# Sharing a PSUM bank between the key and value second layers of a compression pair, and storing the last prompt tile's rows from SyncE's queue

## The chip, the cores and the metric

The kernel runs on one NeuronCore of a Trainium2 chip. The metric is the device time of one execution in microseconds (us); lower is better. The kernel before takes 892.15 us (median of three runs, 891.99 to 892.65). Every row below comes from one profiled execution of it.

Engines are named as the profile names them: PE is TensorE (PEld its weight loads), DVE is VectorE, ACT is ScalarE, POOL is GpSimd, SP is SyncE. A name with q at its end, such as ACTq, is the instruction queue of that engine, where DMA issues stand.

## What is computed

One inference step of a hybrid decoder layer for 512 prompt tokens and 8 sample sequences of 8 tokens with a past of 4096 rows each. One input projection feeds an attention with three gated branches (compressed, selected, window) and a state-space branch; both are projected, gated, added and normalised. The part that the change touches is the compression of the cached keys and values: 16 rows at a time are taken with the 16 rows behind them, sent through a first layer, a SiLU and a second layer.

```python
def compress(rows, w1, b1, w2, b2, pos):
    B, N = rows.shape[:2]
    nch = N // CMP_STRIDE
    ch = rows[:, :nch * CMP_STRIDE].reshape(B, nch, CMP_STRIDE, N_KV, HEAD_DIM).astype(jnp.float32)
    h_first = jnp.einsum('bcpgd,pdh->bcgh', ch, w1[:CMP_STRIDE])
    h_second = jnp.einsum('bcpgd,pdh->bcgh', ch, w1[CMP_STRIDE:])
    h = h_first[:, :-1] + h_second[:, 1:] + (jnp.einsum('pd,pdh->h', pos, w1) + b1)
    out = jnp.einsum('bcgh,hd->bcgd', jax.nn.silu(h), w2) + b2
    ends = jnp.arange(nch - 1, dtype=jnp.int32) * CMP_STRIDE + (CMP_BLOCK - 1)
    return out, ends
```

It is called for the keys and for the values of all 8 samples (255 compressed rows each, 2 heads of 64). The attention of the samples reads `out`, two samples at a time. The prompt's attention output, multiplied by SiLU(z), goes into the output projection at the end.

## The kernel before, in words

**Stages.** The input projection and the state-space scan come first. Then the 512 prompt tokens are attended in four tiles of 128 (`prompt_tile`, i = 0 to 3), tiles 2 and 3 after the compression has been set up. The eight samples follow in `sample`: `compress` makes the compressed keys and values, `attend(w, store)` attends the pair w of samples 2w and 2w+1. The output stage ends the kernel.

**Compression.** `compress` is a generator of small steps. It goes over half samples j = 0 to 15 (sample b = j // 2, half h = j % 2); within a half, first the keys (kv = 0) and then the values (kv = 1), four steps k = 0 to 3 each. I write K0, V0 for the keys and values of sample 0, K1, V1 for sample 1, and so on. A step of `first_layer` splits its rows into a high and a low part (`evh` on ACT, `evl` on DVE; two buffers each) and runs 12 matmuls of about 256 columns on them, into a PSUM bank with the tag "mm" (two banks: one for K, one for V of a sample). Beside the steps, `compress_rows`/`compress_blocks` transpose the rows of the next half (`xt`, DVE, L892) and issue the gathers of later ones (`gc`, POOL, L1091). After the last step of a sample's keys or values, `silu2` reads the bank (ACT, tile `hs`), takes tanh (`hth`) and multiplies (DVE); `hs` has two buffers, so each is held until its second layer's matmuls have read it.

**The second layer.** `second_layer` takes one tile of the tag "ca", which has one bank. For the keys it runs two matmuls (L1165, four instructions in the profile) and ACT copies the result into `kc` (L1168, shown at L108, the line of the helper `act`); for the values it runs two matmuls (L1173, four instructions) for each half t of the rows and DVE copies each half into `vc` (L1175). `late` holds one pending second layer: K of a sample runs in step k = 1 of its own values, V of a sample in step k = 1 of the next sample's keys. `kc` and `vc` live in the pool "attend" (`self.pb`), which lies on the SBUF that the prompt's pools leave.

**Order.** A planner orders each engine's queue when the kernel is built: it takes the instructions that are ready in a simulated run of its own, those that come first in the program ahead of the others, so that steps of `compress` run between the instructions of prompt tiles 2 and 3. On the chip every queue keeps that order: what waits holds up all that stands behind it on its engine.

**The end of a prompt tile.** For the two attention branches the tile transposes the probabilities P (`p_tr`, L135), copies them to SBUF (`pt`, ACT) and multiplies them with the values (`p_acc`, L1036), once for each of i + 1 blocks of keys; the compressed branch comes last (`pcT`, L1078). DVE multiplies the sum with SiLU(z) into `ast` (L1084) and ACT's queue stores it to DRAM (`aD`, L1085). `aD` is read back by the output stage (L1610).

**After it.** `attend_setup` makes the gates (L1220) and loads `selt` (L1217, SP). `past_gather` gathers the cached rows of the selected branch (tile `g`, POOL, also L1091). `attend(w)` starts with the scores against `kc` of both samples of the pair (L1237). SP also carries the loads `y<-yD` (L1548), which the state-space output reads, and other loads of the output stage.

Of the kernel before, what the change touches and what calls it, by code (L numbers as in the profile page):

```python
# [12 lines left out]
AF = mybir.ActivationFunctionType  # L13
OP = mybir.AluOpType
# [71 lines left out]
def rr(ap, pat, **kw):  # L86
    return ap.rearrange(pat, **kw)


class Hybrid:  # L90
# [899 lines left out]
    def prompt_tile(self, i, KT, kczs, vcp, bt):  # L990

        nc, pp = self.nc, self.pp
        V = nc.vector
# [3 lines left out]
        q0 = i * 128  # L997
# [4 lines left out]
        for br in range(2):  # L1002
            P4s = []
            for g in range(2):
# [3 lines left out]
                for r in range(4):  # L1008
                    p = self.psum("S", [128, 512])
# [14 lines left out]
            for kt in range(i + 1):  # L1024
# [10 lines left out]
                for g in range(2):  # L1035
                    mm = nc.tensor.matmul(acc[gr[g]], self.kvn[:, kt, c0 + g * 64:c0 + (g + 1) * 64], PTs[g][:], start=br == 0 and kt == 0,  # L1036
                                          stop=False, skip_group_check=True)
# [9 lines left out]
        p = self.psum("S", [128, 4, 2, 64])  # L1047
# [4 lines left out]
        pv = rr(p[:], "p r g n -> p (r g) n")  # L1052
# [29 lines left out]
        st = pp.tile([128, 4, 128], F, name="ast", tag="ast", bufs=1)  # L1082
        nc.sync.dma_start(st[:], rr(self.zD[0:4], "r p t -> p r t")[:, :, q0:q0 + 128])
        V.tensor_tensor(st[:], rr(acc[:], "p (r q) -> p r q", r=4), st[:], op=OP.mult)  # L1084
        nc.scalar.dma_start(self.aD[:, :, q0:q0 + 128], st[:])  # L1085


    def gather(self, out, cache, idx):
# [67 lines left out]
                             h == 0 and wj == 0, h == 1 and wj == 15, skip_group_check=True)  # L1156
            yield

    def second_layer(self, kv, sl, out):

        nc, V = self.nc, self.nc.vector
        p2 = self.psum("ca", [128, 2, 128])
        if kv == 0:
            for g in range(2):
                nc.tensor.matmul(rr(p2[g * 64:(g + 1) * 64], "p t d -> p (t d)")[:, 0:255], self.w2[:, 0, :], sl[:, g, :],  # L1165
                                 start=True, stop=True)
            V.memset(out[:, 255:256], 0.0)
            self.act(out[:, 0:255], rr(p2[:], "p t d -> p (t d)")[:, 0:255], AF.Identity, bias=self.kb2[:], scale=0.5)  # L1168
        else:
            for t in range(2):  # L1170
                m = 128 - t
                for g in range(2):
                    nc.tensor.matmul(p2[:m, t, g * 64:(g + 1) * 64], sl[:, g, t * 128:t * 128 + m], self.w2[:, 1, :],  # L1173
                                     start=True, stop=True)
                V.scalar_tensor_tensor(out[:m, t], p2[:m, t], 0.5, self.vb2[:m, :], op0=OP.mult, op1=OP.add)  # L1175

    def compress(self, store):


        late = None  # L1180
        for j in range(2 * NB):
            b, h = divmod(j, 2)
            w = b // 2
            rows = self.compress_half(j + 1, NB) if 0 < j < 2 * NB - 1 else iter(())
            if not h:
                accs = [self.psum("mm", [128, 2, 256]) for _ in range(2)]
            xs = self.xs.pop(0)
            for kv in range(2):
                for k, _ in enumerate(self.first_layer(kv, h, xs[kv], accs[kv])):
                    for _ in range(3 if kv + k == 0 else 2):  # L1190
                        next(rows, None)
                    if k == 1 and late:
                        self.second_layer(*late)
                        late = None
                    if k == 3 and h:
                        if w not in store:
                            store[w] = [self.pb.tile([128, 2] + [256] * (1 - v) + [2, 128] * v, F, name=nm, tag=nm, bufs=1)
                                        for v, nm in enumerate(("kc", "vc"))]
                        sl = self.silu2(kv, accs[kv][:, :, 0:255], 255, self.pw, 2)
                        late = kv, sl, store[w][1][:, :, b % 2] if kv else store[w][0][:, b % 2]  # L1200
                    yield
            for _ in rows:
                pass
        self.second_layer(*late)

    def attend_setup(self):
        nc, A, cp, pb = self.nc, self.A, self.cp, self.pb
# [523 lines left out]
```

## Time and profile before

| what | value |
|---|---|
| median of three runs | 892.15 us (891.99 to 892.65) |
| the profiled execution | 889.58 us, of which the span of the core is 887.8 us |
| PE, PEld busy | 849.6 us (96%), 747.8 us (84%) |
| DVE, ACT, POOL busy | 568.8 us (64%), 426.2 us (48%), 196.0 us (22%) |
| mean granted TensorE clock over the span | 0.981 |
| the chain that ended last | PE 65%, DVE 11%, DMA 7%, issue 5%, POOL 4%, ACT 4%, SP's queue 3% |

The profiled execution lies 2.57 us below the median. The 1.78 us between its time and the span lie around the span. A wait row reads: the engine and line that waited, what it waited for, us in total, times, the longest. A timeline row reads: start in us, length in us, engine, line, instruction, output <- inputs, shapes, count, and in brackets the idle time of the engine before it and what ended that. The granted clock is in shares of full speed: 1.00 is 2.4 GHz, 0.50 is 1.2 GHz.

### The profile page before, as it was taken

The page shows a single profiled execution, that of the slowest core. Times are in us where ns is not written, and L with a number is a line of the kernel's source. Part 1 is how long each engine was busy: PE and PEld are TensorE (multiplying, and loading weights), DVE is VectorE, ACT ScalarE, POOL GpSimd, SP SyncE. Part 2 cuts the span into 40 slices and gives each one's busy share as a digit, 9 for nine tenths or more (in the row PEclk, how much of TensorE's full clock was granted, in tenths as well). Part 3 has the DMA queues.
Part 4 walks back from the last instruction along what each step waited for, and adds up shares of the span by engine and source line. Part 5 has one row for each costly group of instructions (what it writes and reads, how often), then busy time and mean ns, then how long its engine had stood idle before and what let it go on. Part 6 is the DMA issues. An engine that isn't in the chain of part 4 may idle for free.

```text
span 887.8 us, 18479 instructions
## 1 busy us (share of the span) xinstructions
PE 849.6 (96%) x7276; PEld 747.8 (84%) x7276; DVE 568.8 (64%) x1559; ACT 426.2 (48%) x876; POOL 196.0 (22%) x249
## 2 busy tenths in 40 slices
PE   8999999999999988999989999999999979999996
PEld 8999999999999967787757878787878758889885
DVE  3469973855354479988627767766764463448784
ACT  4224462223254365768535656555555565545420
POOL 0322719300042211121211323241321101200000
PEclk9999999999999979999979999999999989999999
DMA  8385526365687352323457746383726164849331
GB/s 279 95 201 165 148 67 193 113 203 150 208 247 239 135 133 96 120 96 120 148 182 216 264 164 261 120 313 116 285 97 238 61 236 145 283 129 277 109 107 48
DMA packets 116039, 151.03 MB, mean 170 GB/s; under 512 B 29352, under 2 KB 93224, under 8 KB 111600
## 3 DMA queue, kind: packets, MB, share of 16 engines
q1 hardware_dynamic: 89072, 65.02, 25.6%
q0 software_dynamic: 17824, 80.16, 25.2%
q10 hardware_dynamic: 9056, 4.67, 1.8%
q8 instruction: 57, 0.93, 0.4%
q14 instruction: 30, 0.25, 0.1%
HBM read 134.02 MB, written 19.93 MB: 173 GB/s over the span
## 4 chain that ended last, share of the span: by engine, by line
PE 65%; DVE 11%; DMA 7%; issue 5%; POOL 4%; ACT 4%; SPq 3%; POOLq 0%; DVEq 0%; ACTq 0%
PE p_mm L130 11%; PE p_mm L129 10%; PE p_mm L131 10%; PE p_tr L135 7%; PE p_S L1237 4%; PE p_ca L129 3%; PE p_ca L131 3%; PE p_ca L130 3%; DVE xt L892 2%; PE p_acc L1246 2%; DMA gc<-in_cache_kv_cmp,idx 2%; PE p_acc L1036 2%; DMA relx<-in_rel_bias 1%; DMA wraw<-in_w_in 1%; DVE evl L121 1%
## 5 line engine op out<-in xcount | busy, mean ns | idle before, releaser
L130 PE MATMUL p_mm<-evl,w1h 128*128 128x256 f32 (+1 forms) x512 | 153.8, 300 | 6.3 <-DVE evl L121 6.2
L129 PE MATMUL p_mm<-evh,w1h 128*128 128x256 f32 (+1 forms) x512 | 151.1, 295 | 1.1 <-ACT w1h L108 0.6
L131 PE MATMUL p_mm<-evh,w1l 128*128 128x256 f32 (+1 forms) x512 | 148.2, 290 | 0.9 <-DVE w1l L121 0.9
L121 DVE TENSOR_TENSOR evl<-xt,evh 128x512 fp32r<-128x512 f32 x128 | 87.0, 684 | 52.1 <-ACT evh L108 51.7
L130 PEld LDWEIGHTS p_mm<-evl,w1h 128*128 128x128 f32 x512 | 98.7, 193 | 24.8 <-DVE evl L121 13.1
L108 ACT ACTIVATE evh<-xt 128x512 fp32r<-128x512 f32 x128 | 80.1, 628 | 79.7 <-PE p_mm L131 75.2
L1091 POOL DMA_INDIRECT gc<-in_cache_kv_cmp,idx x64 | 65.5, 1024 | 206.7 <-DVE xt L892 188.9
L129 PEld LDWEIGHTS p_mm<-evh,w1h 128*128 128x128 f32 x512 | 98.9, 193 | 8.7 <-ACT kt L108 2.4
L131 PEld LDWEIGHTS p_mm<-evh,w1l 128*128 128x128 f32 x512 | 98.6, 193 | 5.8 <-issue 4.1
L892 DVE STREAM_TRANSPOSE xt<-gc 128x256 f32<-128x256 f32 x256 | 90.5, 410 | 5.2 <-DMA gc<-in_cache_kv_cmp,idx 4.6
L131 PE MATMUL p_mm<-xTh,wlo 128*128 128x288 f32 x272 | 81.0, 298 | 0.0
L130 PE MATMUL p_mm<-xTl,whi 128*128 128x288 f32 x272 | 81.0, 298 | 0.0
L129 PE MATMUL p_mm<-xTh,whi 128*128 128x288 f32 x272 | 80.9, 298 | 0.0
L108 ACT ACTIVATE pt<-p_tr 128x512 f32<-128x512 f32 x76 | 43.5, 591 | 29.3 <-PE p_tr L135 29.2
L341 DVE TENSOR_TENSOR wlo<-wraw,whi 128x512 fp32r<-128x512 f32 (+1 forms) x56 | 37.5, 728 | 25.4 <-ACT whi L108 25.4
L1091 POOL DMA_INDIRECT g<-in_cache_kv_slc,idx x32 | 32.6, 1018 | 92.9 <-PE p_acc L1246 65.7
L108 ACT ACTIVATE kt<-p_tr 128x512 f32<-128x512 f32 x72 | 40.7, 594 | 24.2 <-PE p_tr L135 24.2
L130 PEld LDWEIGHTS p_mm<-xTl,whi 128*128 128x128 f32 x272 | 51.3, 189 | 0.2 <-issue 0.2
L129 PEld LDWEIGHTS p_mm<-xTh,whi 128*128 128x128 f32 x272 | 51.3, 189 | 0.2 <-issue 0.2
L108 ACT ACTIVATE whi<-wraw 128x2048 fp32r<-128x2048 f32 (+2 forms) x24 | 37.1, 1563 | 29.9 <-DMA wraw<-in_w_in 9.4
L131 PEld LDWEIGHTS p_mm<-xTh,wlo 128*128 128x128 f32 x272 | 51.4, 189 | 0.0
L135 PE MATMUL p_tr<-cst,P 128*128 128x128 f32 x304 | 47.1, 284 | 0.6 <-ACT P L108 0.5
(527 smaller groups left out, 2105.4 us busy)
## 6 DMA issues: line engine op xcount, KB each, us to landing
wraw<-in_w_in SPq DMA_DIRECT2D x11, 1024.0 KB
wraw<-in_w_in SPq DMA_DIRECT2D x10, 512.0 KB
gD<-zst POOLq DMA_DIRECT2D x16, 288.0 KB, 3.2
tg<-gD SPq DMA_DIRECT2D x16, 288.0 KB
wn<-in_state_win_kv POOLq DMA_DIRECT2D x4, 1024.0 KB, 6.2
wor<-in_w_o SPq DMA_DIRECT2D x8, 512.0 KB
out<-in_state_win_kv SPq DMA_DIRECT2D x8, 504.0 KB
wraw<-in_w_in SPq DMA_DIRECT2D x3, 1056.0 KB
```

Of the source, the lines that this page charges most:

```text
L108: return self.nc.scalar.activation(out, in_, func, **kw)
L121: eng.tensor_tensor(lo, src, hi.bitcast(F), op=OP.subtract)
L129: mm(out, lhi, rhi, start=start, stop=False, **kw)
L130: mm(out, lhi, rlo, start=False, stop=False, **kw)
L131: mm(out, llo, rhi, start=False, stop=stop, **kw)
L135: return self.nc.tensor.transpose(out, in_, self.ident[:k, :k])
L341: (eng or self.nc.vector).tensor_tensor(lo[:, kl, :n], w[:, kl, :n], hi[:, kl, :n].bitcast(F), op=OP.subtract)
L892: self.nc.vector.transpose(out=out, in_=in_)
L1036: mm = nc.tensor.matmul(acc[gr[g]], self.kvn[:, kt, c0 + g * 64:c0 + (g + 1) * 64], PTs[g][:], start=br == 0 and kt == 0, stop=False, skip ...
L1091: self.nc.gpsimd.indirect_dma_start(out=rr(out, "c s v g d -> c (s v g d)"), out_offset=None, in_=src, in_offset=bass.IndirectOffsetOnAxis ...
L1237: mm = self.nc.tensor.matmul(out[r], self.qb[:, w, r], keys[b], start=True, stop=True)
L1246: self.nc.tensor.matmul(acc[r], PT[:, r], vals(b)[:, g * 64:(g + 1) * 64], start=start, stop=stop, skip_group_check=True)
```

## The change

Two things change. In `prompt_tile` the store of `ast` goes to SP's queue for the last tile (i = 3) and stays in ACT's queue for the others. In the compression `second_layer` becomes `second_layers`, which takes a list: it allocates one bank of "ca", gives columns 0 to 254 to the keys and columns 256 to 511 to the values, runs all matmuls of the list and then all copies. `late` becomes a list. For the first sample of a pair (b even) the keys' second layer is no longer run during the sample's own values; it waits and runs together with the values' second layer in step k = 1 of the next sample's keys. For the second sample of a pair (b odd) keys and values still run apart, at the places where they ran. The values' matmuls now all come before both copies, with the head in the outer loop and the half t in the inner one. Their number and shapes are the same.

```diff
@@ prompt_tile
         V.tensor_tensor(st[:], rr(acc[:], "p (r q) -> p r q", r=4), st[:], op=OP.mult)
-        nc.scalar.dma_start(self.aD[:, :, q0:q0 + 128], st[:])
+        (nc.sync if i == 3 else nc.scalar).dma_start(self.aD[:, :, q0:q0 + 128], st[:])
@@ second_layer
-    def second_layer(self, kv, sl, out):
+    def second_layers(self, layers):
 
         nc, V = self.nc, self.nc.vector
-        p2 = self.psum("ca", [128, 2, 128])
-        if kv == 0:
+        p2 = self.psum("ca", [128, 512])
+        pk, pv = p2[:, 0:255], rr(p2[:, 256:512], "p (t d) -> p t d", t=2)
+        for kv, sl, _ in layers:
             for g in range(2):
-                nc.tensor.matmul(rr(p2[g * 64:(g + 1) * 64], "p t d -> p (t d)")[:, 0:255], self.w2[:, 0, :], sl[:, g, :],
-                                 start=True, stop=True)
-            V.memset(out[:, 255:256], 0.0)
-            self.act(out[:, 0:255], rr(p2[:], "p t d -> p (t d)")[:, 0:255], AF.Identity, bias=self.kb2[:], scale=0.5)
-        else:
+                if not kv:
+                    nc.tensor.matmul(pk[g * 64:(g + 1) * 64], self.w2[:, 0, :], sl[:, g, :], start=True, stop=True)
+                    continue
+                for t in range(2):
+                    m = 128 - t
+                    nc.tensor.matmul(pv[:m, t, g * 64:(g + 1) * 64], sl[:, g, t * 128:t * 128 + m], self.w2[:, 1, :],
+                                     start=True, stop=True)
+        for kv, _, out in layers:
+            if not kv:
+                V.memset(out[:, 255:256], 0.0)
+                self.act(out[:, 0:255], pk, AF.Identity, bias=self.kb2[:], scale=0.5)
+                continue
             for t in range(2):
                 m = 128 - t
-                for g in range(2):
-                    nc.tensor.matmul(p2[:m, t, g * 64:(g + 1) * 64], sl[:, g, t * 128:t * 128 + m], self.w2[:, 1, :],
-                                     start=True, stop=True)
-                V.scalar_tensor_tensor(out[:m, t], p2[:m, t], 0.5, self.vb2[:m, :], op0=OP.mult, op1=OP.add)
+                V.scalar_tensor_tensor(out[:m, t], pv[:m, t], 0.5, self.vb2[:m, :], op0=OP.mult, op1=OP.add)
@@ compress
-        late = None
+        late = []
...
-                    if k == 1 and late:
-                        self.second_layer(*late)
-                        late = None
+
+                    if k == 1 and late and (b % 2 or not kv):
+                        self.second_layers(late)
+                        late = []
...
-                        late = kv, sl, store[w][1][:, :, b % 2] if kv else store[w][0][:, b % 2]
+                        late.append((kv, sl, store[w][1][:, :, b % 2] if kv else store[w][0][:, b % 2]))
...
-        self.second_layer(*late)
+        self.second_layers(late)
```

## Rows read from the trace of the kernel before

**Rows 1.** The page's engine totals: busy us, share of the span, instructions.
```profile
PE 849.6 (96%) x7276; PEld 747.8 (84%) x7276; DVE 568.8 (64%) x1559; ACT 426.2 (48%) x876; POOL 196.0 (22%) x249
```

**Rows 2.** Stretches: us; PE, PEld, DVE, ACT, POOL busy (instructions); clock, DMA, GB/s.
```profile
400.00:442.35 42.35, 40.19 (x283) 32.66 (x281) 33.27 (x92) 29.25 (x63) 9.01 (x9) 1.00 0.45 140
442.35:453.20 10.85, 9.48 (x53) 4.05 (x51) 3.93 (x13) 4.83 (x10) 0.00 (x0) 1.00 0.05 10
453.20:466.39 13.19, 10.98 (x45) 8.56 (x45) 3.68 (x15) 3.05 (x6) 3.58 (x4) 0.61 0.90 306
466.39:476.39 10.00, 10.00 (x90) 8.68 (x90) 8.85 (x34) 5.99 (x13) 4.29 (x4) 1.00 0.68 184
```

**Rows 3.** Waits from 442.35 to 466.39 us, all engines.
```profile
POOL g L1091 <- PE p_acc L1078: 19.2, 1, 19.2
DVE ast L1084 <- PE p_acc L1078: 6.8, 1, 6.8
ACT hs L108 <- PE p_ca L1173: 4.5, 1, 4.5
PE p_ca L1173 <- ACT kc L108: 1.9, 1, 1.9
```

**Rows 4.** Timeline of 366 to 474 us, the rows of the second layers.
```profile
373.77 0.65 PE L1165 MATMUL p_ca<-hs,w 128*64 128x255 f32 x4
...
442.35 0.28 PE L131 MATMUL p_mm<-evh,w1l 128*128 128x256 f32 x1
...
453.22 0.69 DVE L1084 TENSOR_TENSOR ast<-p_acc,ast 128x512 f32<-128x512 f32 x1 [6.84 <-PE p_acc L1078]
...
453.94 0.52 ACTq L1085 DMA_DIRECT2D aD<-ast  x1
...
454.50 0.47 ACT L108 ACTIVATE kc<-p_ca,kb 128x255 f32<-128x255 f32 x1 [2.46 <-DVE ml L1401]
...
455.03 0.66 PE L1173 MATMUL p_ca<-w,hs 128*128 128x64 f32 x4 [1.86 <-ACT kc L108]
...
455.73 0.29 DVE L1175 SCALAR_TENSOR_TENSOR vc<-p_ca,vb 128x128 f32<-128x128 f32 x1 [1.56 <-PE p_ca L1173]
...
458.49 1.12 PE L1173 MATMUL p_ca<-w,hs 128*127 128x64 f32 x4
459.64 0.29 DVE L1175 SCALAR_TENSOR_TENSOR vc<-p_ca,vb 127x128 f32<-127x128 f32 x1 [1.23 <-PE p_ca L1173]
459.64 0.69 ACT L108 ACTIVATE hs<-p_mm,hb 128x510 f32<-128x510 f32 x1 [4.50 <-PE p_ca L1173]
...
459.99 1.12 PE L1165 MATMUL p_ca<-hs,w 128*64 128x255 f32 x4 [0.38 <-DVE vc L1175]
...
469.98 0.60 PE L135 MATMUL p_tr<-cst,g 128*128 128x128 f32 x4
```

**Rows 5.** One matmul of the first layer on the chain that ended last: start, us.
```profile
439.95 0.12 PE p_mm L129
```

**Rows 6.** PE's waits over the whole span: the one for gathered rows.
```profile
PE p_tr L135 <- DMA g<-in_cache_kv_slc,idx: 1.2, 1, 1.2
```

**Rows 7.** POOL's queue, timeline: a gather for compression that starts after 442 us.
```profile
470.93 1.47 POOL L1091 DMA_INDIRECT gc<-in_cache_kv_cmp,idx  x1 [12.79 <-DVE xt L892]
```

**Rows 8.** SP's queue, timeline, and ACT's first reader of `y`.
```profile
437.12 0.51 SPq L1217 DMA_DIRECT2D selt<-cst  x1
...
450.86 2.69 SPq L1548 DMA_DIRECT2D y<-yD  x6
...
716.65 4.33 ACT L108 ACTIVATE ah<-y 128x576 fp32r<-128x576 f32 x4
```

**Rows 9.** Uses of `aD`: engine, operation, ns, first and last start.
```profile
L1610 SPq DMA_DIRECT2D a<-aD x4: 430/431/506, 736.6 to 738.1; - x4
```

**Rows 10.** Whose waits ended the idle time ahead of L1175: us, times.
```profile
  PE p_ca L1173: 10.3, 8
```

## The prediction

> **What bounds the kernel now.** I read the page's totals first. PE is busy for 849.6 us of 887.8, DVE for 568.8, ACT for 426.2 [rows 1]: an edit pays here only where it gives PE time back. The totals also count a matmul that runs at half clock as busy, so I went next to the table of stretches around the only place where the second layers stand in anybody's way, the end of prompt tile 3. From 400 to 442 us PE runs 283 matmuls in 42.35 us at clock 1.00, 0.150 us each, the idle time included. From 442.35 to 466.39 it runs 53 + 45 = 98 in 24.04 us; it is idle for 1.37 and then for 2.21 us, and in the second part the granted clock is 0.61, part at 1.2 and part at 2.4 GHz. From 466.39 on it runs 90 in 10 us, without idle time, at 1.00 [rows 2]. What PE did before the clock fell is in the first of the two stretches: no more than the chain of the tile's last blocks, with gaps.
>
> The waits of that stretch and the timeline say why there was nothing else to run. K0's second layer ran at 373.77, but its bank is copied out only at 454.50, behind the tile's end: DVE's L1084 at 453.22, then the store in ACT's queue at 453.94 for 0.52 us [rows 4]. For 80 us K0 holds the only bank of "ca". V0's second layer starts at 455.03, when the bank is free, and its other half at 458.49. Until both have read V0's `hs`, the silu of V1 has no buffer: ACT waits 4.5 us for L1173 [rows 3] and reads V1's bank at 459.64 [rows 4]. Until that read V2 has no bank "mm". So at 442.35 the first layer stops, with the 48 matmuls of K2's first half done, and V2's 48 start after 460. One chain, ca, hs, mm, and PE runs dry at the end of it.
>
> **The change part by part.** *One bank for K0 and V0.* It removes the allocation on which V0 waited. Both second layers run right after sample 1's first steps, long before 442 us; V0's `hs` is free when V1 wants it, V1's silu runs when its first layer is done, and V2's bank comes free some 30 us earlier. No instruction disappears, and the four of V0's first half and four of its second move out of the jam. What PE gets is other work for the gaps: V2's first half (48 matmuls), and, as K1 and V1 no longer block the banks "mm", K2's and V2's second halves (96 more), 144 x 0.12 us [rows 5] = 17.3 us. K2's silu is the next that needs a buffer from K1, and K1's second layer still waits for the bank until the tile's end. What is lost today is bounded by two ways of counting. Idle time and clock: 1.37 + 2.21 + 10.98 x (1 - 0.61) = 7.9 us. Rate: 98 x 0.150 = 14.7 us instead of 24.04, 9.3 us [rows 2]. I take the middle, 8.6 us: the rate has the usual waits in it already, but the mix is not quite the same.
>
> What is late next is the tile's end itself. K0 and V0 are copied only when `kc` and `vc` may be written, and I take that to stay at L1084's end. Then follow K0's and V0's copies, K1's matmuls in the same bank, K1's copy, and only then the scores of `attend(0)`. Priced from rows 4: copies 0.47 by ACT and 2 x 0.29 by DVE, K1's matmuls 0.65 (at full clock, the row of K0), K1's copy 0.47. No row of before has ACT and DVE reading one bank of "ca"; side by side the two copies take 0.58, one after the other 1.05. I take the dearer end, and the chain is 1.05 + 0.65 + 0.47 = 2.2 us; all of it is charged, though first-layer work may cover it. The page "PSUM — Partial Sum Buffer" of the Trainium skill, section "PSUM bank collisions raise a hardware error", says that ScalarE and VectorE must not read one bank and quadrant at the same time, so copies out of a shared bank have to be ordered one after the other; this speaks against sharing, no run here shows it yet, and by it the sum is the one with 1.05, by the other view it would be 0.5 us better.
>
> The tile's end also comes later, as first-layer matmuls stand between its blocks, and with it the gathers of `g`, for which POOL waits 19.2 us [rows 3]. The single wait of PE for such rows is 1.2 us [rows 6]; I charge half of it, 0.6, with ends 0 and, in the rival below, far more.
>
> *The store in SP's queue.* ACT gives up 0.52 us in front of K0's copy [rows 4], part of the stretch counted above, so not counted again. On SP the store waits for L1084. `selt` is issued at 437.12, ahead of it; the loads `y` may have to stand behind it, the first six of them issued at 450.86, and their reader is at 716.65 [rows 8]. `aD` is read at 736.6 [rows 9]. Both covers are over 200 us, so the move costs nothing there. If the planner puts the store ahead of `selt`, the gates (L1220) start some 2 us late; I hold it unlikely, since `selt` is ready 16 us earlier.
>
> *The other pairs.* K2, K4 and K6 move half a sample later, beside V2, V4 and V6; the pairs' scores need the odd sample's keys, which come later still. The values' matmuls no longer wait for the first of two copies; DVE has waited 10.3 us in 8 places for L1173 [rows 10], under other work of PE. Counted at nothing, between -1 (each DVE wait that stands ahead of an `evl`) and +1 us (three times half a copy chain).
>
> The sum: 8.6 - 2.2 - 0.6 = 5.8 us, against 889.58 us of the profiled execution: 883.8. The median lies 2.57 us above it, so 892.15 - 5.8 = 886.35, and I say 886.3.
>
> **The rivals.** *The planner leaves the work where it is.* The queues are ordered in its own simulated run, not by what is free on the chip. If V2 still stands behind L1084, the gaps stay and the change does less than it says: what is left is the 0.56 us from 453.94 to 454.50 and V0's matmuls, 0.66 + 1.12 us, out of the chain [rows 4], some 2.3 us: 889.9. For it: DVE and ACT are in order, and L1084 waits for 6.8 us at the head of DVE's queue [rows 3]. Against it: K0's second layer and K2's first half stand well ahead of the tile's end today.
>
> *Given back.* The time is won in the tail and lost after it: the steps that filled the tail are missing under `attend(0)`, whose chain of small operations needs them. 892, give or take 1.
>
> *Slower: too much filler, and the rows come late.* Place: the stretch between L1084 and the first transposes of `g`, 453.2 to 469.98, 16.8 us of gathering [rows 4]. PE's work for it is 21 of today's 45 matmuls, 3.2 us at 0.150, and what is left of the 144. With x of them used in the tail the rest is (144 - x) x 0.12. If the gathers `gc` for sample 3 stand behind those of `g` in POOL's queue, as today (470.93, [rows 7]), nothing else is to be had, and PE idles for 16.8 - 3.2 - (144 - x) x 0.12; at half clock 4.3 us more, as now. From x = 65 on this eats the gain (4.1 + 4.3 us). With 96 it is 7.8 + 4.3 = 12.1 us, against 9.3 won: slower by 2.8 at most, and I take 2.3: 894.5. Against it: the transposes that release `gc` belong to V2's steps, which come early now, and POOL sits idle for 19.2 us in just that time.
>
> **How the numbers follow.** The forecast has 0.58 (its own range 883 to 889.5), the planner's rival 0.13, given back 0.15, slower 0.14. Faster by over 0.2% (under 890.4 us; about what a measurement of this kernel can tell from no change) is the forecast but for 0.02, and most of the planner's rival, 0.08: 0.65 with a little of the third. The same holds what is left of these, 0.20. Slower is the last but for its mild half and some of the third: 0.15. The range goes from 882.8 (all of 9.3 us won) to 893.0 (given back, and the mild half of slower); outside lie 0.04 below and 0.12 above, with some play.
>
> **What would show it.** Right: L1165 and L1173 of sample 0 stand together before 430 us; the wait of `hs` for L1173 is gone; between the last four L1036 groups of tile 3 there are first-layer matmuls; the granted clock stays near 1.00 between 440 and 470 us; L1084 itself comes later than 453.2 us. The copy of K0 follows L1084 with no store between. Wrong: a new idle stretch of PE, with the clock at 1.2 GHz, that waits for `g` or `gc`; or the stretch unchanged with L1173 early. If PE is full there and the end of the kernel has still not moved, it is the third case.

## The result, and the profile after

The kernel after takes 904.59 us (median of four runs, 896.95 to 906.14) against 892.4 us of the kernel before beside it (four runs): ratio 1.0119, 95% interval 1.009 to 1.0149. (The ratios here and below are those on record with the runs, not quotients of medians; the two medians by themselves stand at 1.0137.) It is slower by 1.2%, where 886.3 us was forecast. Its profiled execution took 905.68 us, with a span of 903.9, 16.1 more than before. Chips differ: on two of them the kernel before itself took 907 us; every ratio below is against the kernel before on the same chip.

Engine totals of the page (busy us, share, instructions), then the four stretches of [rows 2] in the kernel after (us; PE, PEld, DVE, ACT, POOL busy; clock, DMA share, GB/s):

```profile
PE 853.7 (94%) x7276; PEld 752.0 (83%) x7276; DVE 570.5 (63%) x1559; ACT 426.5 (47%) x876; POOL 193.6 (21%) x249
```

```profile
400.00:442.35 42.35, 41.69 (x284) 32.32 (x283) 33.26 (x97) 31.26 (x68) 3.86 (x4) 1.00 0.19 63
442.35:453.20 10.85, 10.85 (x78) 7.91 (x77) 8.54 (x24) 5.64 (x12) 4.36 (x4) 1.00 0.60 193
453.20:466.39 13.19, 12.61 (x91) 10.08 (x90) 7.66 (x20) 5.28 (x10) 4.03 (x5) 1.00 0.22 56
466.39:476.39 10.00, 5.41 (x37) 4.63 (x37) 5.28 (x14) 3.58 (x8) 4.50 (x5) 0.83 1.03 354
```

I call the stretch at the end of tile 3 the jam, and first-layer work that runs in it filler. The jam that the forecast set out to fill is full: 78 + 91 = 169 matmuls where [rows 2] has 98, at clock 1.00. But a new hole stands behind it, in the stretch that was full before: PE is idle for 4.59 of the 10 us. The timeline of the second layers and of the tile's end (start, length, engine, line) shows that the bank did what it was to do:

```profile
379.29 0.65 PE L1167 MATMUL p_ca<-hs,w 128*64 128x255 f32 x4
...
394.00 1.00 PE L1171 MATMUL p_ca<-w,hs 128*128 128x64 f32 x8
...
462.68 0.68 DVE L1084 TENSOR_TENSOR ast<-p_acc,ast 128x512 f32<-128x512 f32 x1
...
466.44 0.46 ACT L108 ACTIVATE kc<-p_ca,kb 128x255 f32<-128x255 f32 x1
...
467.17 0.48 DVE L1180 SCALAR_TENSOR_TENSOR vc<-p_ca,vb 128x128 f32<-128x128 f32 x2
...
468.85 0.65 PE L1167 MATMUL p_ca<-hs,w 128*64 128x255 f32 x4
469.54 0.47 ACT L108 ACTIVATE kc<-p_ca,kb 128x255 f32<-128x255 f32 x1
```

V0's second layer (L1171, was L1173) runs at 394.00, not at 455 and 458 as in [rows 4]. The two copies out of the shared bank run one after the other, 466.44 to 466.90 by ACT and 467.17 to 467.65 by DVE. What fills the hole is in SP's queue, in one wait of PE and on the chain that ended last:

```profile
463.38 0.62 SPq L1085 DMA_DIRECT2D aD<-ast  x1
464.09 0.59 SPq L1223 DMA_DIRECT2D selt<-cst  x1
464.77 20.39 SPq L1554 DMA_DIRECT2D y<-yD  x12
```

```profile
PE p_S L1226 <- DMA selt<-cst: 4.6, 1, 4.6
```

```profile
464.09 10.28 DMA selt<-cst
474.41 1.90 PE p_S L1226 x8
476.31 1.05 PE p_S L1243 x4
```

The store now stands ahead of `selt` in SP's queue and waits there for L1084. `selt` is issued at 464.09, not at 437.12 [rows 8], and lands only 10.28 us later, while the DMA engines are full (share 1.03, 354 GB/s in the last stretch above). The gates (L1226, was L1220) run at 474.41; in the kernel before they ran at 455.62:

```profile
455.62 1.90 PE L1220 MATMUL p_S<-gs,selt 64*128 64x24 f32 x8
457.45 1.11 PE L1237 MATMUL p_S<-kc,qb 128*64 128x256 f32 x2
...
469.33 0.59 PE L1374 MATMUL p_S<-pcs,cst 128*128 128x256 f32 x2
```

The hole costs more than the 4.6 us of waiting. Behind it PE is busy without a gap, but the granted clock is 0.50 for five us and 0.68 for five more (stretches of the kernel after, columns as above):

```profile
475.00:480.00 5.00, 5.00 (x23) 4.19 (x23) 1.85 (x12) 0.00 (x0) 0.00 (x0) 0.50 1.04 385
480.00:485.00 5.00, 5.00 (x30) 4.48 (x29) 1.98 (x7) 1.75 (x4) 0.00 (x0) 0.68 1.02 377
```

With the same bank and no hole (e1 below) the clock is 1.00 in these stretches.

### The profile page after: what moved, and what is told of

Same layout as the page of the kernel before. It is cut to its first block, busy times and chain, and to the rows that moved or that the text cites. A ratio compares the mean times of both kernels' runs of the same rounds, so it can differ in the third digit from the quotient of the medians.

```text
span 903.9 us, 18481 instructions
## 1 busy us (share of the span) xinstructions
PE 853.7 (94%) x7276; PEld 752.0 (83%) x7276; DVE 570.5 (63%) x1559; ACT 426.5 (47%) x876; POOL 193.6 (21%) x249
## 4 chain that ended last, share of the span: by engine, by line
PE 66%; DMA 9%; DVE 8%; issue 8%; POOL 4%; ACT 3%; SPq 2%; DVEq 0%; ACTq 0%; POOLq 0%
PE p_mm L130 10%; PE p_mm L129 10%; PE p_mm L131 10%; PE p_tr L135 8%; PE p_S L1243 4%; PE p_ca L129 3%; PE p_ca L130 3%; PE p_ca L131 3%; DMA gc<-in_cache_kv_cmp,idx 2%; PE p_acc L1252 2%; PE p_acc L1036 2%; DMA g<-in_cache_kv_slc,idx 2%; DMA bt<-vD 1%; PE p_mm L365 1%; DMA wraw<-in_w_in 1%
## 5 line engine op out<-in xcount | busy, mean ns | idle before, releaser
L129 PEld LDWEIGHTS p_mm<-evh,w1h 128*128 128x128 f32 x512 | 99.3, 194 | 15.4 <-issue 8.4
```

What stands on the lines that cost most here:

```text
L129: mm(out, lhi, rhi, start=start, stop=False, **kw)
```

## Two theories

**S, the store.** It costs by holding up `selt`, and with it the gates and `attend(0)`. Its rival Y: the store in SP's queue, or the later loads of `y`, cost by themselves. **C, the chain.** What is won in the jam by the bank is lost because `attend(0)` starts later: the chain of the four attends sets the end. Its rival G: the steps used early are missing later, wherever they are used.

Of each profile I read five points: the first and the last L1084, the softmax product of `attend(0)` (L1374 before, the matmul from `pcs`), `zs` (the first work after the last attend, L1606 before) and the end of the span. The early slip of a profile is how much later its first L1084 comes than the 321.1 us of before.

| profile | first L1084 | last | softmax product | `zs` | end | `zs` to end |
|---|---|---|---|---|---|---|
| before | 321.1 | 453.2 | 469.3 | 804.4 | 887.8 | 83.4 |
| after | 326.3 | 462.7 | 485.9 | 823.3 | 903.9 | 80.6 |
| bank alone (e1) | 324.2 | 459.7 | 474.6 | 810.0 | 890.5 | 80.5 |
| store alone (e2) | 323.9 | 457.2 | 478.9 | 811.2 | 901.4 | 90.2 |
| bank, store on POOL (e3) | 325.0 | 460.7 | 488.1 | 813.7 | 894.3 | 80.6 |
| bank alone again (f1) | 323.8 | 459.3 | 474.5 | 812.8 | 893.3 | 80.5 |
| bank, held from step 41 (f2) | 323.3 | 460.5 | 472.8 | 806.2 | 896.6 | 90.4 |
| bank, held from step 37 (f3) | 325.4 | 455.7 | 468.0 | 805.2 | 888.6 | 83.4 |
| bank, gates early (f4) | 323.1 | 463.6 | 487.1 | 814.5 | 896.0 | 81.5 |
| all, gates early (h1) | 322.8 | 462.5 | 480.6 | 807.8 | 889.4 | 81.6 |
| all, gates early, held (h2) | 324.3 | 456.4 | 465.6 | 800.4 | 890.4 | 90.0 |

The last column goes with the number of matmuls that stand behind `zs` in PE's queue: 413 in after, e1 and h1, 435 in before and f3, 454 or 455 in e2, f2 and h2. The planner sets that order when the kernel is built, so a short last column is not time that the chip saved: the other matmuls have run ahead of `zs`.

## The experiments

**Each half alone.** The kernel after with the store back in ACT's queue:

```diff
-        (nc.sync if i == 3 else nc.scalar).dma_start(self.aD[:, :, q0:q0 + 128], st[:])
+        nc.scalar.dma_start(self.aD[:, :, q0:q0 + 128], st[:])
```

> The shared bank alone; the last tile's store goes back to ACT's queue. Theory S (the loss is the store standing ahead of the load of selt in SP's queue, so that the first scores of attend(0) start some 10 us late): selt is issued before 440 us as in the kernel before, PE has no wait for selt, no stretch of half clock after the tile's end, 886 to 890 us. Theory G (given back: steps of the compression that run ahead in the tile's tail are missing under the later attends, whatever selt does): selt early as well, but 893 to 898 us, with idle PE of 5 us or more between 500 and 700 us and again near 800 us.

The kernel before with only the store moved (the same line the other way):

> The second layers of the kernel before; only the last tile's store goes to SP's queue. Theory S: selt is issued behind the store at about 454.6 us and lands 5 to 10 us later while the gathers of g fill the DMA engines; PE waits for it at L1220, 896 to 902 us. Theory G: no more than 1 us away from the kernel before, 891 to 894 us.

Measured: the bank alone 894.96 us, +0.36% (0.17 to 0.55); the store alone 900.9 us, +0.84% (0.57 to 1.11). Neither gains, and the two add up to the +1.2%. The bank alone came out in the range of theory G (893 to 898 us), not of S, so the store is not all of it. The store alone shows the same three rows as the kernel after (SP's queue, PE's wait):

```profile
457.89 0.62 SPq L1085 DMA_DIRECT2D aD<-ast  x1
458.60 0.59 SPq L1217 DMA_DIRECT2D selt<-cst  x1
```

```profile
PE p_S L1220 <- DMA selt<-cst: 7.6, 1, 7.6
```

7.6 us of waiting, and 0.84% of 892 us is 7.5 (the medians are 8.9 us apart). In the bank alone the copies and scores after the tile stand in queues with first-layer work (timeline):

```profile
459.68 0.68 DVE L1084 TENSOR_TENSOR ast<-p_acc,ast 128x512 f32<-128x512 f32 x1
...
460.39 0.52 ACTq L1085 DMA_DIRECT2D aD<-ast  x1
...
461.50 0.63 ACT L108 ACTIVATE evh<-xt 128x512 fp32r<-128x512 f32 x1 [1.71 <-PE p_mm L131]
...
462.88 0.63 ACT L108 ACTIVATE evh<-xt 128x512 fp32r<-128x512 f32 x1 [0.76 <-DVE evl L121]
...
463.42 0.46 ACT L108 ACTIVATE kc<-p_ca,kb 128x255 f32<-128x255 f32 x1
...
465.87 0.65 PE L1167 MATMUL p_ca<-hs,w 128*64 128x255 f32 x4
...
466.57 0.47 ACT L108 ACTIVATE kc<-p_ca,kb 128x255 f32<-128x255 f32 x1
...
466.77 1.07 PE L1226 MATMUL p_S<-gs,selt 64*128 64x24 f32 x8
...
467.77 0.65 PE L1243 MATMUL p_S<-kc,qb 128*64 128x256 f32 x4
```

K0's copy comes 3.1 us after L1084's end (460.36), behind two `evh` that wait for PE; K1's copy ends 6.7 us after it, where I had priced that chain at 2.2.

**The store on other queues.** The store of the last tile on POOL, with the bank:

```diff
-        (nc.sync if i == 3 else nc.scalar).dma_start(self.aD[:, :, q0:q0 + 128], st[:])
+        (nc.gpsimd if i == 3 else nc.scalar).dma_start(self.aD[:, :, q0:q0 + 128], st[:])
```

> The shared bank, with the last tile's store in POOL's queue, off ACT and off SP. Theory S: as the shared bank alone, 886 to 890 us, at most 1 us better for the 0.52 us that ACT gives up; the store stands ahead of the gathers of g on POOL, which wait for the tile's end anyway. Theory G: 893 to 898 us.

Measured 896.66 us, +0.54% (0.23 to 0.84): level with the bank alone within the intervals, so off SP's queue the store's cost is gone or nearly so. The 886 to 890 us of S were missed here too. Then `selt` on ACT, the store left on SP:

```diff
-        self.selt_dma = nc.sync.dma_start(rr(selt[:], "p q r -> p (q r)"), A["cst2"][0:64, a:b])
+        self.selt_dma = nc.scalar.dma_start(rr(selt[:], "p q r -> p (q r)"), A["cst2"][0:64, a:b])
```

> The whole change, with the load of selt in ACT's queue instead of SP's, so that the store cannot stand ahead of it. Theory S: no wait of PE for selt, 886 to 891 us although the store is on SP. Theory G: 893 to 898 us.

Measured 909.99 us, +2.04% (1.74 to 2.34). Both theories missed it. The loads of `y` no longer stand behind `selt`, and ACT's queue:

```profile
479.99 0.54 ACTq L1223 DMA_DIRECT2D selt<-cst  x1
480.64 1.15 ACT L108 ACTIVATE evh<-xt 128x512 fp32r<-128x512 f32 x2 [13.65 <-DMA y<-yD]
```

ACT stands for 13.65 us, by the profile for a load of `y`, and `selt` is issued only then. This one moved the wait and does not separate S from Y; why that issue waits for `y` is open.

**Taking `selt` out of the way.** `selt` is loaded, and the gates are made, ahead of prompt tile 2, in memory of the prompt's pool; the loads of `y` are queued behind the store.

```diff
             self.compress_setup()
+            self.gates()
             for i in range(EARLY, 4):
...
-        (nc.sync if i == 3 else nc.scalar).dma_start(self.aD[:, :, q0:q0 + 128], st[:])
+        self.selt_dma = (nc.sync if i == 3 else nc.scalar).dma_start(self.aD[:, :, q0:q0 + 128], st[:])
```

(`gates` holds the lines from `selt` to `gr` that stood in `attend_setup`; the second edit is what queues `y` behind the store.) The store alone with this:

> The kernel before with the last tile's store in SP's queue, and the load of selt and the gates made ahead of prompt tile 2, so that nothing of attend(0) stands behind the store; the loads of y stay behind it. The store alone, with selt behind it, cost 0.84% (0.57 to 1.11). Theory S (it costs only by holding up selt): -0.3 to +0.2% against the kernel before. Rival Y (the store itself, or the later loads of y): +0.6 to +1.1%.

The whole change with this, on three chips:

> The whole change, with the load of selt and the gates moved ahead of prompt tile 2, so that the last tile's store stands in SP's queue with nothing before it that attend(0) needs; the loads of y are kept behind the store. Theory S (the store costs only by holding up selt): the time falls to that of the bank alone or a little under it, as 1.9 us of gates leave the path too, 892 to 896 us. Rival (the store in SP's queue costs by itself, or by what it does to the loads of y): 900 to 906.

> The whole change with the same. Theory S: the cost of the bank alone, +0.3 to +0.6%. Rival Y: +0.9 to +1.4%, as the kernel after.

> The whole change with selt and the gates ahead of prompt tile 2, once more. If PE shows no waits for issue in this profile: theory S with C gives the cost of the bank alone, +0.3 to +0.6%; if it shows them (3 us and more), -0.6 to -1.2%, as in the last group. A third outcome, a gain without such waits, would mean that the gates on the path were part of the bank's cost.

Measured: the store alone (g1) +0.09% (-0.16 to 0.35), where it cost 0.84 with `selt` behind it. The whole change -1.05% (-1.31 to -0.79; e6) and -0.87% (-1.21 to -0.52; g2) on the two chips where PE showed waits for issue (last section), a gain that neither theory had forecast, and +0.22% (0.05 to 0.39; h1) on one where it showed none. SP's queue and the gates in h1:

```profile
339.03 0.51 SPq L1217 DMA_DIRECT2D selt<-cst  x1
...
344.66 1.07 PE L1220 MATMUL p_S<-gs,selt 64*128 64x24 f32 x8
...
463.21 0.61 SPq L1086 DMA_DIRECT2D aD<-ast  x1
463.92 22.24 SPq L1558 DMA_DIRECT2D y<-yD  x16
```

The store and the loads of `y` stand as in the kernel after, and h1 is level with the bank alone or a little faster: that is S, and against Y. One rival is left. No run has the gates early with the store on ACT and `y` in its old place, so a gain of the early gates by themselves, which would hide a price of the store, is not excluded. Against it stands the wait of 7.6 us for `selt` in the store alone, which is as long as the store's cost.

**The kernel after once more**, on the chip of the store alone (g1) and of the second of the three (g2):

> The kernel after on the same ground: both theories +0.9 to +1.5% against the kernel before.

926.48 us, +1.88% (1.22 to 2.54), with 12.4 us of waits for issue of PE; more than expected, and no clean price of the store. With the gates early the same change took 898.4 us on that chip.

**Holding the filler back.** The bank alone, with the first layer's matmuls from a given step on queued behind `attend(0)`'s first scores:

```diff
+            self.fl += 1
+            with self.tc.issue_after(self.scores.ins) if 32 + 4 <= self.fl < 64 else ExitStack():
...
-        self.pair_mm(p[:], [kc[:, b] for b in range(2)], w)
+        mm = self.pair_mm(p[:], [kc[:, b] for b in range(2)], w)
+        if w == 0:
+            self.scores = mm
```

(4 holds from step 37 on, 8 from step 41 on.) First on a chip with waits for issue:

> The bank alone, and from V2's second half step on (step 41 of the compression: K2's second half and all that follows) the first layer's matmuls are queued behind attend(0)'s first scores. V2's first half may still fill the tile's end. Theory C (the end is set by the chain of attend(0) to attend(3), and the filler that stands in PE's queue between L1084 and the first scores delays it, 453.2 to 465.8 before, 459.7 to 467.8 with the bank alone, the softmax product 469.3 against 474.6): the chain starts 3 to 6 us earlier than with the bank alone and the time falls by as much, to 888 to 892 us. Rival G (steps used early are missing under attend, wherever they were used): no gain, 893 to 897.

> As the one that holds the first layer back from step 41 on, but from step 37 on, so that V2's first half stands behind the scores too, as it does in the kernel before; only V0's second layer has left the tile's end. Theory C: the chain starts earliest of all, but PE has nothing to fill the jam with, so that its 8 us of loss come back: 889 to 893. Rival G: as the kernel before, 891 to 893.

Measured +0.09% (-0.14 to 0.33) and -0.98% (-1.33 to -0.63). Then on one without, beside the bank alone:

> The bank alone again, beside the three below, since the runs of the last group were taken where PE, DVE and ACT showed waits for issue in the attends (PE 6.4 us in 16 places of the kernel before, none in its first profile), which blurs a few us. Both theories: 0 to 0.5% above the kernel before.

> The bank alone with the first layer from step 41 on queued behind attend(0)'s first scores, on the same ground as the bank alone. From the first L1084 to the softmax product of attend(0) it took 148.2 us in the disturbed profile, 150.4 for the bank alone, 148.2 before. Theory C (the start of attend(0)'s chain sets the end): 2 us less than the bank alone, so level with the kernel before or 0.2% under it. Rival G (work used early is missing later, wherever): as the bank alone or worse.

> The same held back from step 37 on. The chain of attend(0) started 141.3 us after the first L1084 in the disturbed profile, 7 us ahead of the kernel before. Theory C: faster than the kernel before, by 3 to 7 us unless PE's own work becomes the bound: ratio 0.992 to 0.997. Rival G: 0.998 to 1.004.

Measured: the bank alone 896.76 us, +0.64% (0.41 to 0.86); held from step 41 895.32, +0.23% (0.11 to 0.36); held from step 37 889.25, -0.37% (-0.61 to -0.13). The less filler may run ahead of the scores, the better: that is C's order, though the step from 41 fell between the two forecasts and the interval of the last one still touches G's 0.998. The bank held from step 37 is faster than the kernel before on either chip (and so than the kernel after). The stretches (columns as above) show that it is not C alone. The kernel before:

```profile
440.00:480.00 40.00, 36.41 (x232) 26.27 (x231) 21.12 (x76) 17.14 (x34) 7.87 (x8) 0.87 0.59 183
480.00:680.00 200.00, 195.77 (x2141) 163.97 (x2141) 136.12 (x414) 112.10 (x224) 55.82 (x55) 1.00 0.57 209
680.00:880.00 200.00, 193.01 (x1647) 166.00 (x1646) 117.20 (x290) 93.59 (x175) 14.53 (x14) 0.98 0.50 157
```

The bank alone (e1):

```profile
440.00:480.00 40.00, 39.42 (x302) 32.09 (x299) 30.09 (x89) 19.98 (x40) 15.54 (x16) 1.00 0.68 233
480.00:680.00 200.00, 192.18 (x2074) 158.87 (x2073) 130.78 (x402) 109.21 (x215) 50.57 (x52) 1.00 0.58 207
680.00:880.00 200.00, 188.50 (x1624) 160.87 (x1623) 115.93 (x287) 93.85 (x179) 14.65 (x14) 0.97 0.51 165
```

The bank held from step 37 on (f3):

```profile
440.00:480.00 40.00, 36.86 (x243) 27.82 (x242) 24.25 (x84) 17.54 (x36) 12.67 (x13) 0.87 0.75 242
480.00:680.00 200.00, 198.56 (x2147) 165.13 (x2145) 137.40 (x412) 114.08 (x226) 55.99 (x55) 1.00 0.59 213
680.00:880.00 200.00, 194.05 (x1642) 167.01 (x1641) 117.88 (x289) 93.26 (x175) 14.10 (x13) 0.97 0.49 157
```

Idle time plus busy time times one minus the clock is what PE loses. Before: 3.59 + 36.41 x 0.13 = 8.3, then 4.2, then 6.99 + 193.01 x 0.02 = 10.9. The bank alone: 0.6, 7.8, 17.2. So the jam gives 7.7 us, near the 8.6 of the forecast, and the rest of the span takes 3.6 + 6.3 = 9.9 back. In the second profile of the bank alone (f1) the same sums are 0.7, 10.8, 17.2. Held: 7.9, 1.4, 11.8: the jam is as it was, and 2.8 us come from 480 to 680, where PE now has steps to run. The held kernel has the later pairs' second layers as the change makes them, and loses 13.2 us behind 480 where the kernel before loses 15.1; so those pairs are hardly where the bank alone loses it. I read it as G's loss: the steps spent in the jam are those missing later. Whether the earlier start of `attend(0)` adds to it (C) these three do not separate, as the held kernel has both.

**The gates early, with the bank, the store on ACT** (the first edit of the gates, without the second):

> The bank alone with the load of selt and the gates moved ahead of prompt tile 2, which takes eight matmuls, 1.9 us, out of PE's queue between the tile's end and the first scores. Theory C: 2 us less than the bank alone. Rival G: the same as the bank alone, as PE's work is the same.

Measured 897.82 us, +0.69% (0.40 to 0.98), level with the bank alone. Of the gates it tells little: the loads of `y` moved ahead, and ACT waited 6.1 us for one of them, as in e4. But it is a test of C, and so is the store on POOL (e3). In both the softmax product of `attend(0)` comes some 13 us later than in the bank alone (table), with a hole of PE in the jam, and yet they take no more than 0.05 and 0.18 points longer, which the intervals do not tell from nothing. Their stretches, first f4, then e3:

```profile
440.00:480.00 40.00, 35.83 (x233) 27.97 (x233) 23.93 (x66) 17.12 (x32) 8.94 (x10) 0.91 0.57 197
480.00:680.00 200.00, 194.95 (x2111) 162.10 (x2111) 133.58 (x417) 113.39 (x223) 53.30 (x54) 1.00 0.56 196
```

```profile
440.00:480.00 40.00, 36.59 (x240) 29.08 (x238) 24.84 (x68) 16.09 (x31) 13.72 (x14) 0.91 0.71 232
480.00:680.00 200.00, 195.75 (x2116) 162.73 (x2116) 134.81 (x420) 113.83 (x225) 53.09 (x54) 1.00 0.56 199
```

By the same sum they lose 7.4 and 6.7 us up to 480, where the bank alone loses 0.7 and 0.6, and 5.1 and 4.3 us from there to 680, where it loses 10.8 and 7.8. Behind 680 all of them lose 17 to 19 us. What is not used in the jam is not missing later: that is what G says, and a late start of `attend(0)` alone did not move the end.

**Both levers.** The whole change, gates early, held from step 37 on:

> The whole change with the gates early, and the first layer from step 37 on queued behind attend(0)'s first scores. Theory C with S: the bank's gain of the kernel that holds back from step 37 (-0.37%, -0.61 to -0.13) or some 2 us more, as the gates leave the path: -0.6 to -0.2%. Rival Y: +0.2% or more.

> The same with the first layer from step 37 on queued behind attend(0)'s first scores. Theory C: below the kernel before on either ground, -0.8 to -0.2%; where no waits for issue are seen it is also 0.5 to 1% below the one that holds nothing back. Rival G: level with the one that holds nothing back.

Measured -0.70% (-1.04 to -0.35) with waits for issue, +0.18% (-0.01 to 0.38) without; there it was to be 0.5 to 1% better than h1 and is level with it. The table says why: `zs` comes at 800.4, 7.4 us ahead of h1, but it takes 90.0 us from there to the end instead of 81.6, with 454 matmuls behind `zs` instead of 413. C alone fails here.

**The kernel before once more.**

> The kernel before, unchanged, profiled a second time. In the first profile the first L1084 stood at 321.1 us; in the profiles of the kernel after and of the three with a part of the change it stood at 322.6 to 326.3, although PE's queue is the same up to K0's second layer. If that slip is a difference between executions, this profile has its first L1084 anywhere from 321 to 326 and the rest moves with it; if it belongs to the changed kernels, it stands at 321 again, within 0.5.

The first L1084 stood at 324.0, 2.9 us later than in the first profile. So an early slip of 3 us comes without the change, though on another chip; I take that much of the slip in the table to belong to the execution. The kernel before took 906.61 us there, for a reason of its own (last section).

## Why the prediction was wrong

- **Bank, what it removes: right.** L1167 and L1171 of sample 0 run before 430, the wait of `hs` is gone, first-layer work stands between the last blocks, the clock is 1.00 to 466 us, L1084 comes later. The gain in the jam was 7.7 us against 8.6.
- **"Both covers are over 200 us, so the move costs nothing there": the step that cost most.** `y` and `aD` were covered; `selt` was not. I named the case and held it unlikely since `selt` was ready 16 us earlier on the chip. The queue's order is made in the planner's run, and the store comes first in the program; that this is why the planner put it first is my reading, no run shows it. I priced the case at some 2 us. The gates came 18.8 us late (455.6 to 474.4): 5.2 of early slip, 4.3 of a later tile end, 4.7 of first-layer work and copies that stand ahead of them in the bank alone too, and 4.6 of the wait for `selt`. The store alone costs 7.5 us of time. The 2 us left out how long `selt` takes to land once the gathers have begun, and the clock of 0.50 behind the hole.
- **8.6 us won in the jam, carried whole to the end: the step that failed in the bank's half.** The sum has no term for the steps that are then missing under the attends. PE lost 9.9 us more from 480 to 880 us than in the kernel before, against the 7.7 that it gained, and the bank alone is 0.36 and 0.64% slower. That PE is busy for 849.6 of 887.8 us did not make time given back to it in one place time at the end. The rival "given back" named the mechanism, at 0.15; it should have been the forecast of this half.
- **"The tile's end also comes later": the term was mis-sized.** I charged 0.6 us, by a wait for gathered rows. From the first to the last L1084 it takes 132.1 us before and 135.5 in the bank alone: 3.4 us. The softmax product comes 5.3 us later: 3.1 of early slip, plus 3.4, less 1.2 that the shorter chain from L1084's end gives (15.4 us before, 14.2). How much of it reaches the end is not shown; e3 and f4 say that little of it needs to.
- **The rivals.** The new idle stretch with a low clock, which I had given as a sign of being wrong, came, but PE waited in it for `selt`. "Too much filler" did not come: in the bank alone PE's waits for `g` are 2.3 us in 2 places over the whole span (1.2 us in one before), and none from 440 to 500 us. That rival's sum also counts 21 matmuls twice: the 21 of the 45 from 453.2 to 466.39 are first-layer work, which is already in the 144. The other 24 are second layers, gates and scores, 16 of them without V0's, or 2.4 us and not 3.2.
- **The copies of the shared bank** ran one after the other, as the dearer end assumed and as the Trainium skill asks for ("PSUM — Partial Sum Buffer", section "PSUM bank collisions raise a hardware error"): 466.44 to 466.90 us by ACT and 467.17 to 467.65 by DVE in the kernel after. But the chain after L1084 took 6.7 us in the bank alone, not 2.2: I had priced its instructions and not the `evh` ahead of them.

Open: why the bank alone costs +0.36 and +0.64% over all runs, while the profile of e1 shows -0.4 us from the first L1084 to the end (566.7 before, 566.3) and that of f1 +2.8. A price of the bank to the microsecond can't be read from single profiles.

## What to carry to other kernels

Before a store is moved to another queue, list everything that will stand behind it there by the order that the scheduler makes, and price the late load by how long it takes when the DMA engines are full. Work pulled forward into a hole is worth something only if nothing lacks that work later: look for the waits that it covers today. Holding filler behind the chain's first step was worth more here (-0.37%) than filling the hole (+0.36 and +0.64%).

## What was not expected of the hardware

On two of the chips, in all eight profiles taken there, PE waits for "issue" inside the dense runs of 128x64 matmuls; in the profiles from the other chips, the first of before among them, it never does. PE's waits over the span and the timeline at one such place, in the second profile of the kernel before:

```profile
PE p_acc L1246 <- issue: 5.6, 14, 0.5
```

```profile
498.27 0.34 PE L1246 MATMUL p_acc<-g,pt 128*32 128x64 f32 x6 [0.40 <-issue]
...
499.02 0.31 PE L1246 MATMUL p_acc<-g,pt 128*32 128x64 f32 x4 [0.41 <-issue]
```

In this stretch a gap of 0.4 us stands after every four to six matmuls. Times of the profiled executions on these chips go with the amount of PE's waits for issue: 12.4 us in the 927 us of g4, 5.0 to 8.3 in those at 906 to 907, 2.9 to 3.3 in those at 897 to 902. They are not the whole of it: the two profiles of the kernel before differ by 17.0 us of span, and these waits are 8.3. So the ratios taken there say as much about these chips as about the change, and I rest no price on them. What PE waits for there is open.

The same load of `selt` landed in 5.6 us at most when issued at 339.03 (h1; the gates ran at 344.66), and took 10.28 us in the kernel after, issued at 464.09 with the DMA engines full.
